# Values weighed in fp32 by two column tiles, products in another order of banks, and attention in a fixed order

## The chip, the cores and the metric

The kernel runs on one core of a Trainium2 chip. The metric is device microseconds (us) of one execution; smaller is better. The engines are named as the profile names them: PE (TensorE, matrix products), DVE (VectorE), ACT (ScalarE), POOL (GpSimd) and SP (SyncE, which issues DMAs). Products are accumulated in PSUM, which PE writes in banks of 512 fp32 columns; DVE, ACT and POOL work between PSUM and SBUF.

## The reference

Two layers of a trunk with three gated branches are applied to 512 latent tokens and 128 context tokens, 640 rows of 1024 channels. All is fp32. One layer, cut to what matters here:

```python
q, k, v, z_a, cb, cc, cx, z_b, fx, z_c, g = split(h @ w_in)
y_a = attn(q, k, v) * silu(z_a)            # 8 query heads, 2 kv heads, head_dim 64
y_b = (cb * dwconv3(cc * cx)) * silu(z_b)  # 512 channels
y_c = Re(fft2(fx)) * silu(z_c)
gates = sigmoid(g)                         # three of 1024 channels
merged = sum(gates[i] * (y_i @ w_branch[i]))
x = LN(alpha * x + gate * (merged @ w_o)) * ln_g + ln_b

# attention of a block of 128 latent queries: keys of the block, its two neighbours, and 128 cached context keys
p = softmax(concat([q @ k * 64**-0.5 (masked), sink]))[..., :-1]
y = p @ v
```

Context tokens attend to the 128 context keys of the prompt only. Keys and values of the context are outputs, too.

## The kernel before

**Precision.** Most products are made from fp32 data cut into a rounded part and a remainder, both of type fp32r; three products (high by high, high by low, low by high) stand for one. A product of 512 weight rows with 320 token columns is 12 matmuls of 128x320. The function `split` does the cut: a copy on ACT gives the high half, a subtraction on DVE the low half (L72).

**Order of work.** The kernel is written as a list of jobs. `run()` goes through it and, ahead of the jobs, loads raw weight tiles (six live at a time, on SP's queue) and splits them (five live at a time). The framework then moves instructions of an engine ahead of others where its own schedule finds that better, unless an instruction is pinned with `tc.keep_in_program_order`: pinned instructions of one engine keep the order in which the program emits them.

**Attention.** Tokens are five tiles of 128: t = 0 to 3 latent, t = 4 context. A unit is a pair (t, kv). `scores` makes, per query head g, a score block of 128 queries by W keys (W = 384, 512, 512, 384; 128 for the context) in PSUM (L651, L662), adds the mask and takes the row's maximum on DVE in one instruction (L654), makes the negated maximum nm (L669, L670), takes the exponential on ACT with a row sum (L676), and, after the reciprocal rc on DVE (L680), scales P by rc on POOL (L682). `values` turns P block by block: four transposes fill a bank (L700), `split` brings it to SBUF as pT, and two matmuls weigh it with VS, whose 128 columns are the high and the low half of 64 channels (L705, L706). The accumulated bank `po` then holds the parts by the high and the low half of the values in different partitions; ACT copies one to yt, DVE adds the other, and the result is multiplied into sz, the SiLU gate. Score, pt, po and x banks come from one pool of four banks (`aux`); scores of unit u+2 are made right after the values of unit u, so P has two buffers by unit.

**The products beside it.** Between units stand the `fills`: the products of the conv branch's input projections. A `Pair` makes two column blocks c0, c1 for 640 tokens by seven products instead of eight (sums of weights and of activations, as in Strassen's scheme). A product goes to one of three accumulators, x, y or z, and after it an evacuation follows: ACT's copy (`keep`, `last_y`) or DVE's addition (`plus`) into the rows gc and gd (gs and ga in `Gates`, a subclass of the same scheme in the gating stage that follows the Fourier stage). Accumulators y and z are halves of one tile, yz, in two banks. Sums of raw weights, s1 among them (which is accumulated by a DMA of POOL's queue), are formed on DVE. There are 8 pairs and 56 products in the attention stage of a layer.

**Output projection.** `oproj(t, n)` makes half n of 512 columns of tile t from 24 matmuls (L1185 to L1187), `residual(t, n)` adds it to x and takes statistics, `finish(t)` is the layer norm; `load_x(t)` loads x.

Of the kernel before, what the change touches and what calls it, by code (L numbers as in the profile page):

```python
# [10 lines left out]
F32R = mybir.dt.float32r  # L11
# [7 lines left out]
NT = 5  # L19
# [15 lines left out]
def body(nc, tc, I, O, ctx):  # L35
# [275 lines left out]

    def transposed(xn, nm, pin=False):
# [224 lines left out]
    def layer(l):  # L537
# [12 lines left out]
        def begin():  # L550
# [3 lines left out]
            S["VS"] = KV[:, 3072:4608].rearrange("p (b v s d) -> p b v s d", b=6, v=2, s=2)  # L554
# [36 lines left out]
        def keys_values():  # L591
# [13 lines left out]
            for i, (a, n, o) in enumerate(((0, 2, 0), (2, 3, 3))):  # L605
# [3 lines left out]
                s = pv[:, :n * 128].rearrange("p (b v d) -> p b v d", v=2, d=64)  # L609
                split(VS[:, o:o + n, :, 0], VS[:, o:o + n, :, 1], s)  # L610
            split(VS[:, 2, :, 0], VS[:, 2, :, 1], cv[:, 0:128].rearrange("p (v d) -> p v d", d=64))
# [25 lines left out]
        def scores(u):  # L637
            def body():
                t, kv = u // 2, u % 2
                nm = f"{l}{t}{kv}"  # L640
                Q, KS, P = S["Q"], S["KS"], S["P"][:, u % 2]
                tok = slice(t * 128, (t + 1) * 128)
                b0, b1 = WINDOW[t] if t < 4 else (5, 6)
                W = (b1 - b0) * 128
                keys = slice(b0 * 128, b1 * 128)
                mx = small(f"mx{nm}")
                if t < 4:
                    for g in range(4):
                        ps = aux(f"s{nm}{g}")
                        for i in range(2):  # L650
                            nc.tensor.matmul(ps[:, :W], lhsT=Q[:, kv * 4 + g, tok], rhs=KS[:, kv, i, keys],  # L651
                                             start=i == 0, stop=i == 1)
# [3 lines left out]
                                                       accum_out=mx[:, g:g + 1])  # L656
                    srcs = [P[:, g, :W] for g in range(4)]
                else:
                    ps = aux(f"s{nm}")
                    for g in range(4):  # L660
                        for i in range(2):
# [702 lines left out]
```

## Time and profile before

| what | us |
|---|---|
| median of three runs | 1288.96 (1285.04 to 1289.44) |
| the profiled execution | 1282.6 |
| its span, from first to last instruction | 1280.8 |
| PE busy | 1198.8 |
| DVE busy | 1011.1 |
| ACT busy | 622.0 |
| POOL busy | 200.1 |
| attention stage, layer 0 (110.82 to 279.78) | 168.96 |
| attention stage, layer 1 (739.44 to 904.96) | 165.52 |

The profile comes from one execution. Busy time counts an engine while an instruction of its own is being executed; on PE neighbouring matmuls overlap, so that the pitch from one start to the next is shorter than one matmul's duration. The granted clock of the whole span is 0.987 of full speed (2.4 GHz). A wait is the idle time of an engine before an instruction, put down to what released it.

### The profile page before, as it was taken

What the parts mean: (1) busy time and instruction counts of PE and PEld (TensorE: products, weight loads), DVE (VectorE), ACT (ScalarE), POOL (GpSimd) and SP (SyncE); (2) the same over time, 40 slices, a digit from 0 to 9 for tenths busy, and PEclk for the clock granted to TensorE, in tenths of its full rate; (3) what the DMA queues carried; (4) which work ended last, traced back from release to release, by engine and by line L of the source; (5) the groups of instructions that cost most, each with busy time, mean ns of one, the idle gap of its engine ahead of it and who ended that gap; (6) DMA issues with size and microseconds to landing.
All of it is one profiled execution on the core that took longest, in us unless ns stands there. A gap on an engine that the chain in (4) does not pass through costs nothing. (4 is left out here: it accounts for less than half of the span.)

```text
span 1280.8 us, 20819 instructions
## 1 busy us (share of the span) xinstructions
PE 1198.8 (94%) x7772; PEld 1134.2 (89%) x7772; DVE 1011.1 (79%) x1855; ACT 622.0 (49%) x1236; POOL 200.1 (16%) x204
## 2 busy tenths in 40 slices
PE   6999888989999999999989979998999999999997
PEld 4899778889889999999779978888999999999986
DVE  5689878868899996777777988888789974667766
ACT  4455566545544344563244656665455443446310
POOL 2011542400000000000230145241000000000001
PEclk9999999999999999999989999999999999999998
DMA  9821213243344543363412311214324533324431
GB/s 355 306 69 35 74 42 80 61 118 106 94 145 142 172 124 92 105 184 127 169 70 70 75 42 50 75 50 125 102 72 132 164 94 97 108 75 140 165 115 66
DMA packets 65812, 143.64 MB, mean 112 GB/s; under 512 B 7792, under 2 KB 8368, under 8 KB 65456
## 3 DMA queue, kind: packets, MB, share of 16 engines
q1 hardware_dynamic: 57504, 125.35, 29.4%
q0 software_dynamic: 7632, 16.68, 7.1%
q8 instruction: 61, 1.00, 0.3%
q14 instruction: 39, 0.32, 0.1%
q10 hardware_dynamic: 576, 0.30, 0.1%
HBM read 136.77 MB, written 5.52 MB: 111 GB/s over the span
## 5 line engine op out<-in xcount | busy, mean ns | idle before, releaser
L682 POOL TENSOR_SCALAR P<-P,rc 128x384 f32<-128x384 f32 (+2 forms) x80 | 114.5, 1447 | 125.5 <-DVE rc L680 98.6
L509 PE MATMUL p<-act,hlw 128*128 128x256 f32 (+1 forms) x256 | 80.5, 314 | 0.0
L511 PE MATMUL p<-act,hlw 128*128 128x256 f32 (+1 forms) x256 | 79.7, 311 | 0.0
L510 PE MATMUL p<-act,hlw 128*128 128x256 f32 (+1 forms) x256 | 79.2, 309 | 0.0
L1185 PE MATMUL o<-wo,act 128*128 128x512 f32 (+1 forms) x168 | 63.7, 381 | 2.3 <-ACT hv L331 2.3
L1186 PE MATMUL o<-wo,act 128*128 128x512 f32 (+1 forms) x168 | 63.4, 379 | 0.0
L1187 PE MATMUL o<-wo,act 128*128 128x512 f32 (+1 forms) x168 | 62.8, 380 | 0.0
L239 DVE SCALAR_TENSOR_TENSOR moda<-rawm,scond,moda 128x512 f32<-128x512 f32 x84 | 61.2, 744 | 0.4 <-DMA rawm<-in_w_mod 0.4
L69 ACT ACTIVATE gs<-y 128x320 f32<-128x320 f32 x48 | 20.9, 435 | 74.7 <-PE y L827 74.6
L509 PEld LDWEIGHTS p<-act,hlw 128*128 128x128 f32 x256 | 48.4, 189 | 1.1 <-issue 0.8
L511 PEld LDWEIGHTS p<-act,hlw 128*128 128x128 f32 x256 | 48.2, 188 | 0.0
L510 PEld LDWEIGHTS p<-act,hlw 128*128 128x128 f32 x256 | 48.2, 188 | 0.0
L75 DVE TENSOR_TENSOR gs<-pb,gs 128x640 f32<-128x640 f32 x16 | 13.2, 824 | 38.0 <-PE pb L511 38.0
L676 ACT ACTIVATE P<-P,nm 128x384 f32<-128x384 f32 (+1 forms) x64 | 42.0, 657 | 0.1
L654 DVE CUSTOM_DVE_ANT_0 P<-s,mask 128x384 f32<-128x384 f32 (+1 forms) x64 | 38.4, 615 | 3.8 <-PE s L651 3.7
L72 DVE TENSOR_TENSOR pT<-pt,pT 128x512 fp32r<-128x512 f32 x60 | 40.6, 682 | 0.6 <-ACT pT L69 0.5
L69 ACT ACTIVATE hlw<-raww 128x512 fp32r<-128x512 f32 x40 | 25.0, 631 | 32.1 <-PE p L511 19.3
L705 PE MATMUL po<-pT,KV 128*128 128x512 f32 x60 | 25.7, 428 | 15.6 <-ACT pT L69 15.5
L147 DVE TENSOR_TENSOR hlb<-rawb,hlb 128x512 fp32r<-128x512 f32 x48 | 33.0, 687 | 9.3 <-ACT hlb L69 9.1
L509 PE MATMUL pb<-sya,hlb 128*128 128x256 f32 (+1 forms) x128 | 40.1, 313 | 0.1
L69 ACT ACTIVATE hlb<-rawb 128x512 fp32r<-128x512 f32 x48 | 30.1, 627 | 20.3 <-PE z L827 8.0
L509 PE MATMUL pb<-yc,hlb 128*128 128x256 f32 (+1 forms) x128 | 39.9, 312 | 0.0
(1131 smaller groups left out, 3874.2 us busy)
## 6 DMA issues: line engine op xcount, KB each, us to landing
rawm<-in_w_mod SPq DMA_DIRECT2D x48, 512.0 KB, 5.7
rawg<-in_w_in SPq DMA_DIRECT2D x72, 256.0 KB, 3.3
rawb<-in_w_branch SPq DMA_DIRECT2D x48, 256.0 KB, 3.1
raww<-in_w_in SPq DMA_DIRECT2D x40, 256.0 KB, 4.5
rawo<-in_w_o SPq DMA_DIRECT2D x32, 256.0 KB, 4.2
rawgc<-in_w_in SPq DMA_DIRECT2D x24, 256.0 KB, 2.8
rawgd<-in_w_in SPq DMA_DIRECT2D x24, 256.0 KB, 2.9
rawgf<-in_w_in SPq DMA_DIRECT2D x24, 256.0 KB, 2.9
```

Of the source, the lines that this page charges most:

```text
L69: nc.scalar.activation(out, in_, AF.Copy)
L72: nc.vector.tensor_tensor(out=out, in0=a, in1=b, op=ALU.subtract)
L239: nc.vector.scalar_tensor_tensor(out=acc[:, c], in0=w, scalar=scond[:, k, c:c + 1], in1=acc[:, c], op0=ALU.mult, op1=ALU.add)
L509: nc.tensor.matmul(ps[:, a:b], lhsT=ld.w(0, k), rhs=mh, start=k == 0, stop=False)
L510: nc.tensor.matmul(ps[:, a:b], lhsT=ld.w(0, k), rhs=ml, start=False, stop=False)
L511: nc.tensor.matmul(ps[:, a:b], lhsT=ld.w(1, k), rhs=mh, start=False, stop=k == nk - 1)
L654: nc.vector.tensor_tensor_reduce(out=P[:, g, :W], in0=ps[:, :W], in1=mask[:, mp:mp + W], scale=1.0, scalar=-3e38, op0=ALU.add, op1=ALU.max ...
L676: nc.scalar.activation(P[:, g, :W], srcs[g], AF.Exp, scale=0.125, bias=nm_[:, g:g + 1], accum_out=sm[:, g:g + 1])
L682: nc.gpsimd.tensor_scalar(out=P[:, g, :W], in0=P[:, g, :W], scalar1=rc[:, g:g + 1], scalar2=None, op0=ALU.mult)
L1185: nc.tensor.matmul(ps, lhsT=act[:, t, 0, k], rhs=w[:, 0], start=k == 0, stop=False)
L1186: nc.tensor.matmul(ps, lhsT=act[:, t, 0, k], rhs=w[:, 1], start=False, stop=False)
L1187: nc.tensor.matmul(ps, lhsT=act[:, t, 1, k], rhs=w[:, 0], start=False, stop=k == NK - 1)
```

## The change

Five things are done.

- **Values.** VS holds plain fp32 values. One copy on ACT brings a turned block of both kv heads to pT. `weigh(b)` makes two fp32 matmuls, kv 0 and kv 1, with 64 weight columns each, placed in column tiles (0, 0) and (0, 64) of PE, into the two halves of one bank. The final multiplication reads that bank. The low half of pT (DVE), yt's copy (ACT) and addition (DVE) fall away.
- **Seven products.** Their accumulators come in the order y, z, y, x, y, z, y instead of y, x, z, y, y, y, z; the matmuls of the products of the conv pairs are pinned (those of `Gates` aren't).
- **Attention's order.** The matmuls of scores, transposes and values are pinned as well. Both units of a tile share the steps: scores (t+1, kv 0), two products, scores (t+1, kv 1), six products; then for each block b of that tile the weighing of block b-1, the transposes of b for both kv heads, and one product. P has a buffer for each kv head.
- **Conv.** The first of the three taps is scaled on ACT instead of DVE.
- **Output projection.** All of x is loaded at the begin, and residual(t, 0) follows oproj(t, 0) directly.

```diff
@@ -309,6 +309,9 @@
     def pe(ins):
         tc.keep_in_program_order(ins)
 
+    def pinned(ins):
+        tc.keep_in_program_order(ins)
+
     def transposed(xn, nm, pin=False):
         halves = []
...
@@ -563,7 +565,8 @@
 
         def begin_scores():
             P = big.tile([128, 5120], F32, name=f"P{l}", tag="C")
-            S["P"] = P[:, :4096].rearrange("p (u g k) -> p u g k", u=2, g=4)
+            S["P"] = P[:, :4096].rearrange("p (v g k) -> p v g k", v=2, g=4)
+            S["VS"] = P[:, 4096:4864].rearrange("p (b v d) -> p b v d", b=6, v=2)
         job(begin)
 
         def after_h(f):
...
-            split(VS[:, 2, :, 0], VS[:, 2, :, 1], cv[:, 0:128].rearrange("p (v d) -> p v d", d=64))
+                copy(VS[:, o:o + n], pv[:, :n * 128].rearrange("p (b v d) -> p b v d", v=2, d=64))
+            copy(VS[:, 2], cv[:, 0:128].rearrange("p (v d) -> p v d", d=64))
             nc.vector.tensor_copy(out=cv[:, 128:256], in_=pv[:, 256:384])
             nc.gpsimd.dma_start(out=O["new_v"][l], in_=cv[:, 128:256])
...
@@ -628,42 +630,52 @@
         for c in range(4):
             inproj(l, C_Q + c, use_q(c))
             if c == 0:
+                job(begin_scores)
                 job(after_h(keys_values))
             if c < len(groups):
                 job(groups[c][0])
-        job(begin_scores)
-
-
...
+        def scores(t, kv):
...
+                for i in range(2):
+                    pinned(nc.tensor.matmul(ps, lhsT=S["Q"][:, kv * 4 + g, tok], rhs=S["KS"][:, kv, i, keys],
+                                            start=i == 0, stop=i == 1))
+
+            def some(g0, g1):
+                def body():
+                    P = S["P"][:, kv]
+                    if g0 == 0:
+                        S["mx", u] = small(f"mx{nm}")
+                    for g in range(g0, g1):
                         ps = aux(f"s{nm}{g}")
-                        for i in range(2):
-                            nc.tensor.matmul(ps[:, :W], lhsT=Q[:, kv * 4 + g, tok], rhs=KS[:, kv, i, keys],
-                                             start=i == 0, stop=i == 1)
+                        score(ps[:, :W], g)
                         mp = MASKPOS[t] * 128
                         nc.vector.tensor_tensor_reduce(out=P[:, g, :W], in0=ps[:, :W], in1=mask[:, mp:mp + W],
                                                        scale=1.0, scalar=-3e38, op0=ALU.add, op1=ALU.max,
...
+                        srcs[g] = P[:, g, :W]
+                return body
...
@@ -681,36 +693,44 @@
                 for g in range(4):
                     nc.gpsimd.tensor_scalar(out=P[:, g, :W], in0=P[:, g, :W], scalar1=rc[:, g:g + 1],
                                             scalar2=None, op0=ALU.mult)
-            return body
...
+            def both(*fs):
+                return lambda: [f() for f in fs]
+            return [some(0, 2), both(some(2, 4), softmax)] if t < 4 else [both(context, softmax)]
+
+        def values(t):
+            b0, b1 = WINDOW[t] if t < 4 else (5, 6)
+            pT = {}
+
+            def turn(b):
+                pT[b] = tmp(f"pT{l}{t}{b}")
+                for kv in range(2):
+                    pt = aux(f"pt{l}{t}{b}{kv}")
                     for g in range(4):
...
+                        pinned(nc.tensor.transpose(pt[:, g * 128:(g + 1) * 128],
+                                                   S["P"][:, kv, g, (b - b0) * 128:(b - b0 + 1) * 128], ident))
+                    copy(pT[b][:, kv * 512:(kv + 1) * 512], pt)
+
+            def weigh(b):
+
+                if b == b0:
+                    S["po"] = aux(f"po{l}{t}")
+                for kv in range(2):
+                    pinned(nc.tensor.matmul(S["po"][kv * 64:(kv + 1) * 64], lhsT=S["VS"][:, b, kv],
+                                            rhs=pT[b][:, kv * 512:(kv + 1) * 512], start=b == b0, stop=b == b1 - 1,
+                                            tile_position=(0, kv * 64)))
+
+            def step(b):
+                def body():
+                    if b > b0:
+                        weigh(b - 1)
+                    if b < b1:
+                        turn(b)
+                    else:
+                        sz = S["sz"][:, :, t * 128:(t + 1) * 128]
+                        mul(sz, S["po"].rearrange("p (g q) -> p g q", g=4), sz)
+                return body
+            return [step(b) for b in range(b0, b1 + 1)]
 
         def use_za(c):
@@ -794,13 +814,15 @@
                     return lambda k, z: S["T"][i][:, z, k]
                 self.steps = [
                     (Load([s1, a11, a12, a22], [hl(a11, [], 1)]), "y", old(0, 0), self.keep(0, 0)),
+                    (Load([], [hl(s1, [], 5)]), "z", new(0), self.keep(1, 1)),
+                    (Load([], [Sum(add, s1, s1, a11), hl(s1, [], 6)]), "y", new(1), self.keep(0, 1)),
                     (Load([], [hl(a12, [], 2)]), "x", old(0, 1), self.plus(0, 0)),
-                    (Load([], [hl(s1, [], 5), Sum(add, s1, s1, a11)]), "z", new(0), lambda out: None),
-                    (Load([], [hl(s1, [], 6), Sum(sub, a11, s1, a22), Sum(add, a12, a12, s1, [s1])]), "y", new(1),
-                     self.keep(0, 1)),
-                    (Load([], [hl(a11, [a11], 7)]), "y", new(2), self.third),
-                    (Load([], [hl(a22, [a22], 4)]), "y", lambda k, z: act[:, :, z, k, 64:128], self.last_y),
-                    (Load([], [hl(a12, [a12], 3)]), "z", old(1, 1), self.last_z)]
+                    (Load([], [Sum(sub, a11, s1, a22), Sum(add, a12, a12, s1, [s1]), hl(a11, [a11], 7)]), "y", new(2),
+                     self.plus(1, 1)),
+                    (Load([], [hl(a12, [a12], 3)]), "z", old(1, 1), self.last_z),
+                    (Load([], [hl(a22, [a22], 4)]), "y", lambda k, z: act[:, :, z, k, 64:128], self.last_y)]
+
+            pin = staticmethod(pinned)
 
             def place(self, bank):
...
@@ -841,15 +863,11 @@
                     add(quarter(self.G[i], half), out, quarter(self.G[i], half))
                 return then
 
-            def third(self, out):
-                self.keep(1, 1)(out)
-                self.plus(1, 1)(self.ps["z"][:, :320].rearrange("p (t i) -> p t i", i=64))
+            def last_z(self, out):
+                self.plus(0, 1)(out)
 
             def last_y(self, out):
                 copy(quarter(self.G[1], 0), out)
-
-            def last_z(self, out):
-                self.plus(0, 1)(out)
                 self.done(*self.G)
 
@@ -864,8 +882,7 @@
                 mul(u[:, 1:513], cc[:, 0:512], cx[:, 0:512])
                 mul(u[:, 514:642], cc[:, 512:640], cx[:, 512:640])
                 y = S["cy"] = row(f"cy{l}{j}")
-                nc.vector.tensor_scalar(out=y[:, 0:641], in0=u[:, 1:642], scalar1=convw[:, l, j, 1:2], scalar2=None,
-                                        op0=ALU.mult)
+                nc.scalar.activation(y[:, 0:641], u[:, 1:642], AF.Copy, scale=convw[:, l, j, 1:2])
                 for i in (0, 2):
                     nc.vector.scalar_tensor_tensor(out=y[:, 0:641], in0=u[:, i:i + 641], scalar=convw[:, l, j, i:i + 1],
@@ -887,10 +904,15 @@
                 if fill:
                     fill.pop(0).emit(1)
 
+        def several(fs):
+            for f in fs:
+                job(f)
+
         if l == 0:
             job(groups[0][1])
-        job(scores(0))
+        several(scores(0, 0))
         gating(0)
+        several(scores(0, 1))
         if l == 0:
             job(groups[0][2])
             job(groups[1][1])
@@ -899,17 +921,19 @@
             job(groups[1][2])
         job(begin_sums)
         job(sums(0))
-        job(scores(1))
         gating(2)
         job(sums(1))
-        for u in range(10):
-            job(values(u))
-            if u == 0:
-                gating(3)
-                job(last_sum)
-            if u + 2 < 10:
-                job(scores(u + 2))
-            fills(6 if u else 2)
+        gating(3)
+        job(last_sum)
+        for t in range(NT):
+            for f in values(t):
+                job(f)
+                fills(1)
+            if t + 1 < NT:
+                several(scores(t + 1, 0))
+                fills(2)
+                several(scores(t + 1, 1))
+                fills(6)
         fills(99)
 
@@ -1030,6 +1054,8 @@
                 c = C_G + b * 8 + 2 * m
                 super().__init__(f"{l}{b}{m}", c, c + 1, begin, None)
 
+            pin = staticmethod(free)
+
             def place(self, bank):
                 return aux(f"{bank}{self.nm}")
...
@@ -1228,21 +1257,17 @@
             if l == 0:
                 job(lambda: make_h(1, t, S["xn", t], pin))
 
-        job(oproj(0, 0))
-        job(oproj(1, 0))
-        job(oproj(2, 0))
-        job(residual(0, 0))
-        job(residual(1, 0))
+        for t in range(3):
+            job(oproj(t, 0))
+        for t in range(3):
+            job(residual(t, 0))
         for t in range(NT):
-            if t > 1:
-                job(residual(t, 0))
             job(oproj(t, 1))
             job(residual(t, 1))
-            if t < NT - 2:
-                job(lambda t=t: load_x(t + 2))
             if 0 < t < NT - 1:
                 if t + 2 < NT:
                     job(oproj(t + 2, 0))
+                    job(residual(t + 2, 0))
                 next_h(t - 1)
             if t == NT - 1 and l == 0:
                 next_h(t - 1, True)
```

On PE, in the attention stage of layer 0, before: the scores of unit (2, kv 1) (s0210 to s0213; names are layer, t, kv, g) stand among the values of unit (1, kv 1) (po011) and products of the pair c01.

```order
L651 MATMUL s0210_1835<-KV0_553,Q0_552 128x512 x2
L706 MATMUL po011_1790<-pT0112_1816,KV0_553 128x512
L651 MATMUL s0211_1839<-KV0_553,Q0_552 128x512 x2
L705 MATMUL po011_1790<-pT0113_1826,KV0_553 128x512
L651 MATMUL s0212_1843<-KV0_553,Q0_552 128x512 x2
L827 MATMUL yzc01_1869<-tb0_1100,hlgc01p5_1742 128x320 x12
L827 MATMUL yzc01_1869<-tb0_1100,hlgc01p6_1759 128x320 x7
L706 MATMUL po011_1790<-pT0113_1826,KV0_553 128x512
L651 MATMUL s0213_1847<-KV0_553,Q0_552 128x512 x2
L827 MATMUL yzc01_1869<-tb0_1100,hlgc01p6_1759 128x320
L827 MATMUL xc01_1891<-act_109,hlgc01p2_1725 128x320 x12
L827 MATMUL yzc01_1869<-tb0_1100,hlgc01p6_1759 128x320 x4
```

The unit's own transposes (pt0211) stand 22 rows below the last of these, after the transposes and values of unit (2, kv 0). After, the same scores, the six products and the transposes of both kv heads:

```order
L650 MATMUL s0210_1875<-KV0_553,Q0_552 128x512 x2
L650 MATMUL s0211_1879<-KV0_553,Q0_552 128x512 x2
L650 MATMUL s0212_1883<-KV0_553,Q0_552 128x512 x2
L650 MATMUL s0213_1887<-KV0_553,Q0_552 128x512 x2
L849 MATMUL yzc01_1731<-act_109,hlgc01p3_1747 128x320 x12
L849 MATMUL yzc01_1731<-act_109,hlgc01p4_1781 128x320 x12
L849 MATMUL yzd01_1956<-act_109,hlgd01p1_1802 128x320 x12
L849 MATMUL yzd01_1956<-tb0_1132,hlgd01p5_1854 128x320 x12
L849 MATMUL yzd01_1956<-tb0_1132,hlgd01p6_1871 128x320 x12
L849 MATMUL xd01_2012<-act_109,hlgd01p2_1922 128x320 x12
L710 MATMUL pt0210_2031<-ident_90,P0_659 128x128 x4
L710 MATMUL pt0211_2037<-ident_90,P0_659 128x128 x4
```

The scores have moved from beside another unit's values to a place six products ahead of their own transposes.

On DVE, before, around the maxima of unit (2, kv 1) (P0 and mx021 from s0210): the first two rows are the sum sm020 and the reciprocal rc020 of unit (2, kv 0). The first maximum of kv 1 is the row behind the last one shown.

```order
L78 TENSOR_TENSOR sm020_1666<-sm020_1666,es020_1663 128x4
L680 RECIPROCAL rc020_1672<-sm020_1666 128x4
L78 TENSOR_TENSOR gd001_1591<-yzd00_1577,gd001_1591 128x5x64
L147 TENSOR_TENSOR hlgc01p6_1759<-rawgc01s_1390,hlgc01p6_1759 128x512
L72 TENSOR_TENSOR pT0110_1796<-pt0110_1791,pT0110_1796 128x512
L75 TENSOR_TENSOR gd001_1591<-gd001_1591,cy00_1568 128x512
L75 TENSOR_TENSOR gd001_1591<-gd001_1591,cy00_1568 128x128
L147 TENSOR_TENSOR hlgc01p7_1785<-rawgc0110_1410,hlgc01p7_1785 128x512
L72 TENSOR_TENSOR pT0111_1806<-pt0111_1801,pT0111_1806 128x512
L72 TENSOR_TENSOR pT0112_1816<-pt0112_1811,pT0112_1816 128x512
L78 TENSOR_TENSOR gd000_1590<-yzd00_1577,gd000_1590 128x5x64
L147 TENSOR_TENSOR hlgc01p4_1885<-rawgc0122_1575,hlgc01p4_1885 128x512
```

After, the same place:

```order
L681 SCALAR_TENSOR_TENSOR mx020_1805<-mx020_1805,sink_96 128x4
L147 TENSOR_TENSOR hlgd01p5_1854<-rawgd01s_1572,hlgd01p5_1854 128x512
L682 TENSOR_SCALAR nm020_1822<-mx020_1805 128x4
L72 TENSOR_TENSOR es020_1825<-sink_96,mx020_1805 128x4
L78 TENSOR_TENSOR rawgd01s_1572<-rawgd01s_1572,rawgd0110_1591 128x512
L78 TENSOR_TENSOR gc011_1745<-yzc01_1731,gc011_1745 128x5x64
L72 TENSOR_TENSOR rawgd0110_1591<-rawgd01s_1572,rawgd0122_1714 128x512
L78 TENSOR_TENSOR sm020_1828<-sm020_1828,es020_1825 128x4
L692 RECIPROCAL rc020_1834<-sm020_1828 128x4
L662 ISA P0_659,mx021_1874<-s0210_1875,mask_107 128x512
L662 ISA mx021_1874 128x1
L662 ISA P0_659,mx021_1874<-s0211_1879,mask_107 128x512
```

The maxima of kv 1 now follow rc of kv 0 directly, and the subtractions for pT (L72) are gone.

On PE, at the turn from tile 3 to tile 2's second half in layer 0's output projection, with what each row waits for, before:

```order
L318 MATMUL tr100_6506<-ident_90,xn10_6439 128x128 [waits Activation_49]
L318 MATMUL tr100_6506<-ident_90,xn10_6439 128x128 x3
L318 MATMUL tr101_6511<-ident_90,xn10_6439 128x128 [waits DVE_49]
L318 MATMUL tr101_6511<-ident_90,xn10_6439 128x128 x3
L1185 MATMUL o02512_6591<-wo02_6280,act_109 128x512 [waits Activation_49]
```

and after:

```order
L321 MATMUL tr100_6409<-ident_90,xn10_6338 128x128 [waits Activation_49]
L321 MATMUL tr100_6409<-ident_90,xn10_6338 128x128 x3
L321 MATMUL tr101_6414<-ident_90,xn10_6338 128x128 [waits DVE_49]
L321 MATMUL tr101_6414<-ident_90,xn10_6338 128x128 x3
L1214 MATMUL o02512_6489<-wo02_6172,act_109 128x512 [waits DVE_49]
```

The first matmul of o02512 waits for DVE where it waited for ACT.

## Rows read from the trace of the kernel before

**Rows 1.** The page: the span, and PE's busy time, its share and instructions.

```profile
span 1280.8 us, 20819 instructions
...
PE 1198.8 (94%) x7772; PEld 1134.2 (89%) x7772; DVE 1011.1 (79%) x1855; ACT 622.0 (49%) x1236; POOL 200.1 (16%) x204
```

**Rows 2.** Waits of PE: waiting line, releaser; total us, times, longest.

```profile
PE po L705 <- ACT pT L69: 15.5, 10, 3.8
PE yzc L827 <- ACT gc L69: 15.3, 13, 2.2
...
PE yzd L827 <- ACT gd L69: 3.8, 5, 1.0
PE y L827 <- ACT ga L69: 3.4, 4, 1.5
...
PE o L1185 <- ACT hv L331: 2.3, 2, 1.2
PE y L827 <- ACT gs L69: 2.2, 7, 0.5
```

**Rows 3.** Windows of both stages: us, each engine's busy time (x), PEclk.

```profile
110.82:279.78 168.96, 147.61 (x930) 135.94 (x928) 139.13 (x287) 99.87 (x218) 56.43 (x53) 0.99 0.26 71
739.44:904.96 165.52, 146.11 (x905) 135.09 (x903) 134.58 (x281) 98.98 (x216) 61.27 (x54) 0.97 0.26 72
```

**Rows 4.** Timeline of PE, products: start, us of the row.

```profile
1028.27 1.92 PE L827 MATMUL y<-act,hlg113p 128*128 128x320 f32 x12
1030.03 1.92 PE L827 MATMUL y<-act,hlg112p 128*128 128x320 f32 x12
```

**Rows 5.** Timeline of PE, output projection of layer 1.

```profile
1226.45 0.39 PE L1185 MATMUL o<-wo,act 128*128 128x512 f32 x1
1226.67 0.39 PE L1186 MATMUL o<-wo,act 128*128 128x512 f32 x1
```

**Rows 6.** Timeline of PE, transposes of P.

```profile
115.92 1.03 PE L700 MATMUL pt<-ident,P 128*128 128x128 f32 x8
116.71 0.37 PE L509 MATMUL p<-act,hlw 128*128 128x256 f32 x1
```

**Rows 7.** Window of the first stage, products of L827 alone.

```profile
110.82:279.78 168.96, 104.30 (x637) 96.25 (x637) 0.99 0.26 71
```

**Rows 8.** Groups by form: busy us, mean ns of one, idle before.

```profile
L682 POOL TENSOR_SCALAR P<-P,rc 128x512 f32<-128x512 f32 x32 | 54.2, 1717 | 39.6 <-DVE rc L680 20.8 <-ACT hlgd10p L69 7.4 <-ACT pT L69 4.1
...
L682 POOL TENSOR_SCALAR P<-P,rc 128x384 f32<-128x384 f32 x32 | 45.9, 1445 | 66.9 <-DVE rc L680 58.7 <-PE yzc L827 4.1 <-PE s L662 4.0
...
L72 DVE TENSOR_TENSOR pT<-pt,pT 128x512 fp32r<-128x512 f32 x60 | 40.6, 682 | 0.6 <-ACT pT L69 0.5
...
L676 ACT ACTIVATE P<-P,nm 128x512 f32<-128x512 f32 x32 | 22.6, 710 | 0.0
...
L654 DVE CUSTOM_DVE_ANT_0 P<-s,mask 128x512 f32<-128x512 f32 x32 | 21.4, 679 | 2.9 <-PE s L651 2.9
```

**Rows 9.** Timeline of PE, an fp32 product in column tiles.

```profile
80.82 0.34 PE L511 MATMUL p<-act,hlw 128*128 128x384 f32 x1
81.09 1.92 PE L464 MATMUL modp<-rawm,scond 128*32 128x512 f32 x16
82.94 0.44 PE L651 MATMUL s<-KV,Q 128*128 128x384 f32 x1
```

**Rows 10.** Timeline of VectorE, then of ACT, where Exp's table is loaded.

```profile
808.48 0.16 DVE L670 TENSOR_SCALAR nm<-mx 128x4 f32<-128x4 f32 x1
...
809.14 1.28 ACT L676 ACT_TABLE_LOAD   x1
```

**Rows 11.** Timeline of POOL, scaling of unit (1, kv 0), layer 1.

```profile
764.26 7.54 POOL L682 TENSOR_SCALAR P<-P,rc 128x512 f32<-128x512 f32 x4 [7.43 <-ACT hlgd10p L69]
```

**Rows 12.** Windows around two waits of PE: columns as in rows 3.

```profile
745.00:752.00 7.00, 3.17 (x13) 2.87 (x13) 6.01 (x11) 6.81 (x18) 2.01 (x1) 0.76 0.18 47
662.00:668.00 6.00, 6.00 (x35) 6.00 (x34) 5.46 (x9) 3.94 (x10) 3.32 (x2) 0.62 0.02 8
```

More of the change, by code (lines that the diff above doesn't have):

```diff
@@ L633, in layer, with score @@
                 job(groups[c][0])
[L634 to L648 removed]
+        def scores(t, kv):
+            u = t, kv
+            nm = f"{l}{t}{kv}"
+            tok = slice(t * 128, (t + 1) * 128)
+            b0, b1 = WINDOW[t] if t < 4 else (5, 6)
+            W = (b1 - b0) * 128
+            keys = slice(b0 * 128, b1 * 128)
+            srcs = {}
+            def score(ps, g):
+                for i in range(2):
[7 more added lines that the diff above has]
+                    for g in range(g0, g1):
                         ps = aux(f"s{nm}{g}")
[L650 to L652 removed]
+                        score(ps[:, :W], g)
                         mp = MASKPOS[t] * 128
@@ L655, in body, with context, softmax @@
                                                        scale=1.0, scalar=-3e38, op0=ALU.add, op1=ALU.max,
[L656 to L661, printed above, removed]
-                            nc.tensor.matmul(ps[:, g * 128:(g + 1) * 128], lhsT=Q[:, kv * 4 + g, tok],
-                                             rhs=KS[:, kv, i, keys], start=i == 0, stop=i == 1)
-                    nc.vector.tensor_reduce(out=mx, in_=ps.rearrange("p (g k) -> p g k", g=4),
-                                            axis=mybir.AxisListType.X, op=ALU.max)
-                    srcs = [ps[:, g * 128:(g + 1) * 128] for g in range(4)]
+                                                       accum_out=S["mx", u][:, g:g + 1])
+                        srcs[g] = P[:, g, :W]
+                return body
+            def context():
+                ps = aux(f"s{nm}")
+                for g in range(4):
+                    score(ps[:, g * 128:(g + 1) * 128], g)
+                    srcs[g] = ps[:, g * 128:(g + 1) * 128]
+                S["mx", u] = small(f"mx{nm}")
+                nc.vector.tensor_reduce(out=S["mx", u], in_=ps.rearrange("p (g k) -> p g k", g=4),
+                                        axis=mybir.AxisListType.X, op=ALU.max)
+            def softmax():
+                P, mx = S["P"][:, kv], S["mx", u]
                 nm_ = small(f"nm{nm}")
@@ L826, in body @@
                         for i, (z, y) in enumerate(((0, 0), (0, 1), (1, 0))):
-                            nc.tensor.matmul(out, lhsT=ld.w(z, k), rhs=moving(k, y), start=first and k == i == 0,
-                                             stop=k == 3 and i == 2, skip_group_check=True)
+                            self.pin(nc.tensor.matmul(out, lhsT=ld.w(z, k), rhs=moving(k, y), start=first and k == i == 0,
+                                                      stop=k == 3 and i == 2, skip_group_check=True))
                     then(out.rearrange("p (t i) -> p t i", i=64))
```

34 lines of the change are left out of this document (4 added, 30 removed).

## The prediction

> **What bounds the kernel now.** I read the head of the page first: a span of 1280.8 us with PE busy for 1198.8 of it [rows 1], so a gain must come from the 82 us in which PE is not busy, or from work that leaves PE. The waits of PE come next, since they name what PE stood for [rows 2]: values matmuls waiting for ACT's copy of pT 15.5 us, products waiting for a bank's evacuation into gc 15.3 and gd 3.8, and, in the gate pairs after the stage, ga 3.4 and gs 2.2; the output projection waits 2.3 for hv. Then the windows of the two attention stages [rows 3]: 168.96 and 165.52 us, in which PE is busy 147.6 and 146.1. Busy time overlaps between neighbouring matmuls, so I count by pitch, from start to start. Twelve 320-column matmuls take 1030.03 − 1028.27 = 1.76 us [rows 4]; a 512-column one .225 to .23 us [rows 5]; eight transposes .79 [rows 6], and with the step to their neighbours .109 each. The first stage holds 637 product matmuls [rows 7], at .1465 each 93.3 us; 120 transposes 13.1; 60 values matmuls 13.9; with the scores' 64 matmuls 12.0 and the gating projections' 49, of two widths, 7.1, at pitches between these, it comes to 139.5. PE waits some 29.5 us there, and by the same count 29.7 in the second stage, which has half of the gating. These 59 us are what the change plays for; VectorE, at 139 and 135 us of work in the two windows, is nearly as full as PE there, and I expected that to matter most.
>
> **Values.** Per block and kv head the VectorE half of the split goes: 60 × .68 = 40.6 us [rows 8]; with 20 additions of the same shape, 13.6 by the same mean, VectorE sheds 54 us; ACT loses 20 copies. Eight conv scalings leave VectorE for ACT as well. All this lies beside PE's work and is worth nothing by itself, only through waits that get shorter. On PE, 120 matmuls of .23 are replaced by 30 pairs, each pair weighing one block for both kv heads. An fp32 product in column tiles is in the trace: eight calls, 16 records, from 81.09 to the next row at 82.94 [rows 9]. That is four rounds of four tiles side by side, at most 1.85 / 4 = .46 each with the changes of tiling in them. The first record is .09 late too: the row before began at 80.82, and its 384 columns take .176 at the pitch per column of rows 4. A pair is two rounds: .92, the late start .09, and a little for an exit that is spread over four rounds there and over two here: 1.05 us, against 4 × .231 = .92. Hence +.12 × 30 = +3.7 us. From below, with nothing for changes and rounds of .43, −2; from above, if the two tiles don't run together, +26 (a rival).
>
> The Trainium skill, "TensorEngine Tiling (Array Packing)", Tiling Modes, Key Properties, says that a change of tiling mode drains TensorE, a rule against this change, which makes 60 of them; the trace agrees, with the .09 at 81.09, and by it the sum stays as it is.
>
> **The fixed order in attention.** This is the main term. Before, a unit's scores are issued two units ahead of its values and whatever is ready fills PE. The order shows unit (2, kv 1) scored, then six products, two of them already in flight, and a whole other unit's transposes before its own pt0211. After, both units of a tile are scored just ahead of it: scores kv 0, two products, scores kv 1, six products, then at once the transposes of both. PE reaches kv 1's transposes 1.85 + 3.52 + 1.85 + 10.56 + .44 = 18.2 us after it starts on kv 0's scores (eight matmuls of .231, products of 1.76, four transposes of .109).
>
> P must be ready by then. I walk the order of VectorE after the change with durations of before. kv 0: four masked maxima at .68 [rows 8], behind the scores, end at 3.7; with the gc addition, one split and two small operations, nm is there at 5.15. Exp then loads its table, 1.28 us, which needs nm: behind a split of ACT it began .5 after nm's end [rows 10], I take .25: 6.7; four exps of .71 [rows 8] end at 9.6, rc at 10.1. POOL scales four pieces, each between 1.45 (the mean at 384 keys) and 1.72 (at 512) [rows 8]: 10.3 to 16.5 at 1.55. So kv 0 is in time. But the order puts kv 0's sm and rc, which wait for these exps, ahead of kv 1's masked maxima on VectorE. These therefore begin at 10.1, not at 5.4 when their scores start; they end at 12.5, nm follows behind two splits and an addition at 15.1, exps 15.3 to 18.2, rc 18.7, scaling 18.9 to 25.0. PE stands 25.0 − 18.2 = 6.8 us. One unit of before has four scalings in 7.54 [rows 11], which would make it 8; with chains as short as the rows allow (no table, no split between) it is 4. I take 6.8 for the two tiles of 512 keys after the first, 4 for the tile of 384 (1.5 to 6: shorter maxima and exps, the same order), nothing for the context tile of 128: 17.6 a layer, 35 in all (20 to 48).
>
> Each such wait costs more than itself. Around a 3.8 us wait PE's granted clock was .76 over 7 us [rows 12], a part of it at the 1.2 GHz level: 7 × .24 = 1.7 us lost, in the window in which the wait itself lies; after a longer wait, .62 over 6 us, or 2.3 [rows 12]. Six stalls at 1.7 are 10 (5 to 20). Inside a tile, weigh(b−1) follows a product of 1.76 us after the transposes, while ACT needs two copies of .59 and may be on a split of .63: .2 us a step, 15 steps a layer, 3 us; as much again for products whose bank or split is late at the start of the stage. That is 12 for both layers (4 to 24). Stage after: 35 + 10 + 12 + 3.7 = 61, against 59 before: +2. What VectorE no longer does is not seen in it, because kv 1's chain is a chain of waits, not of work. The waits for pT (15.5) and gc in the stage do go, but they are exchanged for waits for P.
>
> **The order of products.** Between two products into one bank another bank's product now stands in most places, 1.76 us against a copy of .44. In the stage this is already in the count above; outside it, ga and gs, 3.4 + 2.2 [rows 2], go: −5.6 (−10, if waits too short for a row go as well, to +2, if splits come late in the new order: since the accumulated sum s1 is used a product earlier).
>
> **Output projection and tail.** The order shows o02512 wait for VectorE instead of ACT: two waits of 1.16 for hv [rows 2] go, −2.3 (0 to −3). The first half of tile 4's residual moves ahead of the last matmuls, −1.3, about one row-wide operation of VectorE at the end (0 to −2). All loads of x go out together and earlier, on SP's queue ahead of later weight loads: 0, or +2 if one of those comes late.
>
> **Sum.** +1.9 − 5.6 − 2.3 − 1.3 = −7.3 on the profiled execution of 1282.6 us: 1275.3. The runs' median is 1288.96, 6.4 above it, so 1281.7 as a median.
>
> **The rivals.** *The chain is shorter.* If the maxima of kv 1 don't stand behind rc for as long (kv 0's exps find their table loaded, POOL at 1.45), the stalls are 3.5, 3.5 and 2: 18 us instead of 35, with the clock's share unchanged: −17, 1265. For it: the exps of a unit can follow the unit before without another table load; against it: ACT's sigmoid work stands between units. *P is late by more, slower.* Place: POOL's scaling of kv 1 and the exps ahead of it, in the three tiles of a layer that stall. If four scalings take 7.5 instead of 6.2 [rows 11] and VectorE's queue adds another 1 us, stalls are 9, 9 and 6: +13, and if each costs 3 us of clock instead of 1.7, +8: 1281.7 + 21 = 1303. It decides from the point where each of the six stalls costs 1.2 us more than I put it, which makes the total no gain. For it: the unit at 764.26; against: most scalings in the group's mean are 1.72 and the waits for pT, as long as 3.8 today, vanish. *The column tiles don't run side by side*, since a call is two records and both of one tile may precede the other's: three rounds a pair, +.43 × 30 = +13, 1295; none together, +26, 1308. Against it, the 16 records at 81.09 stand in 1.85 us, four rounds where eight calls one after another would be 16.
>
> By the Trainium skill, "TensorE: Matmul & The Clock Gate", Part 3, The mechanism, matmuls start and end in program order without exception; records taken strictly tile by tile would then make three rounds of a pair. The records at 81.09 speak against that reading. *The products' order does nothing* (the waits for ga and gs stay): 1287, inside my forecast's own range.
>
> **Numbers.** Forecast .47, own range 1268 to 1289; shorter chain .23; later P .18; tiles not together .12. Half a per cent, about what can be told from no change here, is 6.4 us: below 1282.5, above 1295.4. Faster: .24 of the forecast's .47 and all of .23: .47. Same: .21 of the forecast, .02 and .05 of the next two: .28. Slower: .25. The range 1262 to 1303 takes in the shorter chain and the later P.
>
> **What would show it.** Right: among PE's waits the transposes of kv 1 for POOL, two long ones and a middling one per layer, in place of po for pT; po pairs about 1.05 us; rc of kv 0 just ahead of kv 1's maxima; a stage of 165 to 170 us. Wrong: no transposes that wait, stages below 160; or pairs over 1.3 us; or waits of products for their splits above 15 us, which would mean that the fixed order has moved the weight path onto PE's.

## The result, and the profile after

The changed kernel takes 1339.99 us (median of four runs, 1332.45 to 1340.15) against 1288.47: ratio 1.039, interval 1.0349 to 1.0432. It is 51.5 us slower, where 7 us less were forecast. Its profiled span is 57.5 us longer. The head of its page, as [rows 1]:

```profile
span 1338.3 us, 20691 instructions
...
PE 1225.5 (92%) x7772; PEld 1137.5 (85%) x7772; DVE 966.2 (72%) x1761; ACT 623.0 (47%) x1230; POOL 203.4 (15%) x204
```

VectorE shed its work; the span grew. To find where, I cut both executions at the same points of the program: the first product of the gate pairs in each layer, and the first transposes of P in layer 1. The windows of before (us elapsed first, then PE's busy time; PEclk behind POOL's column):

```profile
0.00:353.34 353.34, 316.63 (x2124) 289.42 (x2124) 282.40 (x578) 195.22 (x398) 80.06 (x89) 0.99 0.39 122
353.34:739.44 386.10, 374.22 (x2404) 360.80 (x2404) 317.37 (x532) 173.57 (x326) 36.93 (x35) 0.99 0.40 122
739.44:978.47 239.03, 217.56 (x1396) 204.31 (x1395) 195.96 (x399) 139.84 (x301) 67.62 (x66) 0.98 0.29 79
978.47:1280.80 302.33, 290.44 (x1855) 279.68 (x1854) 215.35 (x349) 113.41 (x211) 15.50 (x15) 0.99 0.37 114
```

and after:

```profile
0.00:376.14 376.14, 326.64 (x2124) 288.64 (x2124) 262.20 (x535) 196.32 (x395) 84.36 (x89) 0.96 0.37 117
376.14:758.03 381.89, 376.10 (x2424) 364.13 (x2425) 314.19 (x533) 174.64 (x329) 38.91 (x35) 0.99 0.40 121
758.03:1035.16 277.13, 230.51 (x1373) 202.30 (x1372) 173.99 (x351) 138.24 (x296) 64.50 (x65) 0.92 0.26 71
1035.16:1338.30 303.14, 292.28 (x1853) 282.44 (x1853) 215.83 (x345) 113.83 (x214) 15.62 (x15) 0.98 0.36 112
```

The two stretches with attention and the conv and Fourier pairs lose 22.8 and 38.1 us. Of those with gates and output projection the first wins 4.2, the second loses 0.8. PE's matmuls in the windows are the same but for 22 gating matmuls of layer 1, some 3.6 us: the change puts them ahead of the first transposes, out of the third window into the second. PE's waits, as [rows 2]:

```profile
PE yzc L849 <- DVE gc L78: 22.2, 12, 3.9
PE yzd L849 <- ACT gd L69: 18.0, 13, 3.3
PE pt L710 <- POOL P L694: 14.0, 7, 9.2
...
PE yzf L849 <- DVE fz L78: 8.4, 10, 1.0
PE yzf L849 <- ACT fz L69: 7.3, 12, 1.0
...
PE yzc L849 <- ACT gc L69: 5.2, 4, 2.0
```

With 2.8 more for yzd behind VectorE, products into yz wait 63.9 us in 55 places; before, the same kinds gave 22.2 (15.3 and 3.8 of [rows 2], 1.6 for yzd behind VectorE, 1.5 for yzf). The waits of po (17.9) and of ga, gs and hv are gone, as forecast. What PE waits for is seen at the first two products of a pair, y and then z (PE, then ACT; start, us):

```profile
260.90 1.98 PE L849 MATMUL yzc<-act,hlgc03p 128*128 128x320 f32 x12
263.46 0.85 PE L849 MATMUL yzc<-tb,hlgc03p 128*128 128x320 f32 x4 [0.59 <-ACT gc L69]
```

```profile
262.97 0.44 ACT L69 ACTIVATE gc<-yzc 128x320 f32<-128x320 f32 x1 [1.75 <-PE yzc L849]
```

The second product writes bank z, into which nothing of this pair had been written. Still it starts when ACT has copied bank y: 2.56 us after the first, where 1.76 is the pitch. All 55 waits stand ahead of the second, third, sixth and seventh product of a pair (15, 14, 12 and 14 of the 24 pairs of both layers); no first, fourth or fifth product waits. Such a wait becomes long where the evacuation itself is queued. At the next example ACT's copy stood behind the conv tap that the change had moved to ACT, and that one waited 2.9 us. The row puts this down to POOL; but the tap reads u, and VectorE, which makes u, ended it just before, at 145.89 (first row):

```profile
145.00 0.89 DVE L75 TENSOR_TENSOR u<-gc,gc 128x512 f32<-128x512 f32 x2
...
145.97 0.83 ACT L885 ACTIVATE cy<-u,convw 128x641 f32<-128x641 f32 x1 [2.88 <-POOL P L694]
146.71 0.42 ACT L69 ACTIVATE gd<-yzd 128x320 f32<-128x320 f32 x1
```

```profile
141.94 1.92 PE L849 MATMUL yzd<-act,hlgd00p 128*128 128x320 f32 x12
147.18 2.42 PE L849 MATMUL yzd<-tb,hlgd00p 128*128 128x320 f32 x12 [3.32 <-ACT gd L69]
```

### The profile page after: what moved, and what is told of

Its sections match the earlier page's. It is cut to its first block, busy times and chain, and to the rows that moved or that the text cites. A ratio compares the mean times of both kernels' runs of the same rounds, so it can differ in the third digit from the quotient of the medians.

```text
span 1338.3 us, 20691 instructions
## 1 busy us (share of the span) xinstructions
PE 1225.5 (92%) x7772; PEld 1137.5 (85%) x7772; DVE 966.2 (72%) x1761; ACT 623.0 (47%) x1230; POOL 203.4 (15%) x204
## 4 chain that ended last, share of the span: by engine, by line
PE 73%; DVE 12%; ACT 7%; issue 3%; DMA 3%; POOL 2%; DVEq 0%; POOLq 0%; ACTq 0%; SPq 0%
PE y L849 13%; PE z L849 6%; PE yzf L849 5%; PE yzc L849 5%; PE yzd L849 5%; PE pb L512 4%; PE pb L514 4%; PE pb L513 4%; PE x L849 3%; PE po L719 2%; PE p L401 2%; PE pt L710 2%; PE p L512 2%; PE p L514 2%; PE p L513 2%
## 5 line engine op out<-in xcount | busy, mean ns | idle before, releaser
L710 PEld LDWEIGHTS pt<-ident,P 128*128 128x128 f32 x240 | 26.8, 141 | 33.1 <-POOL P L694 15.8
L710 PE MATMUL pt<-ident,P 128*128 128x128 f32 x240 | 34.3, 281 | 14.0 <-POOL P L694 14.0
L69 ACT ACTIVATE pT<-pt 128x512 f32<-128x512 f32 x60 | 32.8, 593 | 23.9 <-PE pt L710 23.9
L512 PE MATMUL pb<-syb,hlb 128*128 128x256 f32 (+1 forms) x128 | 40.1, 313 | 0.0
```

The costliest lines, as they stand in the source:

```text
L69: nc.scalar.activation(out, in_, AF.Copy)
L512: nc.tensor.matmul(ps[:, a:b], lhsT=ld.w(0, k), rhs=mh, start=k == 0, stop=False)
L710: pinned(nc.tensor.transpose(pt[:, g * 128:(g + 1) * 128], S["P"][:, kv, g, (b - b0) * 128:(b - b0 + 1) * 128], ident))
```

## The experiments

Theory A: y and z are halves of one tile of PSUM, and the program orders a write to the tile behind every earlier read of it, whichever bank is read. Rivals: B, the fixed order itself; C, late P. Stalls of "76" and "29" us in the expectations are counted from start to start beyond the pitch, over 0.25 us each.

**two_tiles.** In the changed kernel:

```diff
+        turn_of = {}
...
-                    self.two = mmt(f"yz{self.nm}")
-                    return self.two[:, 0:512]
-                return self.two[:, 512:1024]
+                    self.two = mmt(f"yz{self.nm}"), mmt(f"zy{self.nm}")
+                    if turn_of.setdefault(self.nm, len(turn_of)) % 2:
+                        self.two = self.two[::-1]
+                    return self.two[0][:, 0:512]
+                return self.two[1][:, 512:1024]
```

> The changed kernel; the accumulators y and z of a conv or Fourier pair lie in two tiles of PSUM instead of two banks of one tile, and the two tiles change roles from pair to pair. Nothing else differs, and PE's order is the same. Theory A: a product into one bank waits until the other bank has been evacuated, because both banks are one tile and a write to a tile is put behind every earlier read of it; PE's stalls of over 0.25 us ahead of products into yz are 76 us in the changed kernel and 29 in the one before. Then they fall below 25 us and the time falls by 45 to 55, to 1285 to 1295 us. Rival B: the fixed order itself costs the time (nothing can move up into a wait), whatever the tiles: the stalls stay above 60 us, the time at 1325 or more. Rival C: P arrives late, which is what the prediction named: the waits of the transposes for POOL (14 us) are the larger part with what they do to the clock, and the time falls by less than 15 us.

Measured: 1294.05 (ratio to before 1.005, 1.0031 to 1.007), 46 us less than the changed kernel, with PE's order in the attention stages unchanged (around the Fourier pairs some matmuls that aren't pinned moved). All waits ahead of products into y and z fell from 63.9 to 16.5 us. The same two products now stand 1.81 us apart:

```profile
264.34 1.98 PE L853 MATMUL yzc<-act,hlgc03p 128*128 128x320 f32 x12
266.15 1.92 PE L853 MATMUL zyc<-tb,hlgc03p 128*128 128x320 f32 x12
```

Time and waits are those of theory A; B and C fall as the main cause. And the wait that the prediction had named takes part of the place, since PE now gets to the transposes sooner:

```profile
PE pt L710 <- POOL P L694: 36.9, 22, 9.2
PE zyd L853 <- ACT gd L69: 11.2, 8, 2.6
```

**products_free.** The changed kernel with

```diff
-            pin = staticmethod(pinned)
+            pin = staticmethod(free)
```

> The changed kernel with the products of the pairs not pinned; scores, transposes and values stay pinned. Theory A: the waits for the other bank stay in the program, but products of the next pair, in another tile, can move up into some of them: stalls ahead of yz products fall from 76 to about 40 us, time 1300 to 1315 us. Rival B (the fixed order): the time goes back to that of the kernel before, 1285 to 1292. Rival C (late P): no change, 1335 or more.

Measured: 1318.18 (1.0233, 1.0214 to 1.0253). The yz waits fall to 40 us, but the time stays 3 us above A's range: PE's own work grows, since products stand between the two halves of 19 of the 30 value pairs, whose starts take 51.9 us instead of 31.6 (see values_free).

**order_alone.** The kernel before with the list of seven steps, `last_z` and `last_y` of the change.

> The kernel before with only the new order of the seven products (y, z, y, x, y, z, y), nothing pinned, values as before. Theory A: four of seven products follow a product into the other half of the same tile whose evacuation they have to wait for, where it was three before (two of them into the same bank); the framework's freedom hides a part: slower by 5 to 20 us, 1293 to 1308. Prediction's reading (another bank's product covers the evacuation): faster by about 5 to 15, 1273 to 1283. Rival B (only the pins cost): the same within 5 us.

Measured: 1267.44 (0.9841, 0.9824 to 0.9858). The expectation from A is wrong: where nothing is pinned, the order is worth 21 us, more than the prediction's reading gave.

```profile
PE yzc L827 <- ACT gc L69: 9.4, 6, 3.3
...
PE po L705 <- ACT pT L69: 7.2, 6, 4.3
PE yzd L827 <- ACT gd L69: 4.6, 7, 1.4
```

With 1.7 each for yzc and yzd behind VectorE and 0.8 for yzf, yz waits 18.2 (22.2 before), po 7.6 with its second half (17.9), and ga's and gs's 5.6 are gone; waits for split weights in the gate pairs grew from 2.3 to 5.6. That is 16.6, where the two profiled spans differ by 15.9 (the medians by 21). So only 4.0 are waits of products into y and z; most is po's. What the prediction said of the order is seen in the gate pairs, where x, y and z are three tiles.

**before_two_tiles.** The kernel before with two tiles, without the change of roles.

> The kernel before with y and z in two tiles, in its own order of products (y, x, z, y, y, y, z). Theory A: of its three waits per pair two are for the same bank and stay, the last (z behind y) goes: the 29 us of stalls ahead of yz products fall by a third, time 1276 to 1282 us. Rivals B and C: nothing changes, 1285 to 1292, since in this kernel nothing is pinned and P is not late.

Measured: 1273.02 (0.9885, 0.9869 to 0.9901). The time fell by more than A said, but the yz waits didn't fall (22.3 us). The profiled spans differ by 9.5 us, of which po's waits give 3.8 (17.9 to 14.1); the rest is spread over small waits and starts, and this run alone doesn't show its mechanism.

**order_and_tiles.** Both edits in the kernel before, roles changing.

> The kernel before with the new order of the products and with y and z in two tiles that change roles from pair to pair; nothing pinned, values as before. The order alone gave 1267.4 us, two tiles alone 1273.0. If both take away the same waits (a product behind the evacuation of the pair's banks), the two together give little more than the order alone: 1260 to 1267. If the order takes away the waits for the same bank and the tiles those for the other bank, as theory A has it, the gains add: 1250 to 1258. If P's or the weights' chain is the next wait, it ends above 1265.

Measured: 1249.09 (0.9697, 0.9682 to 0.9711): 38 us, where the parts alone gave 21 and 15. They add.

**scores_together.** In two_tiles:

```diff
-            for f in values(t):
+            fs = values(t)
+            for f in fs:
                 job(f)
-                fills(1)
+                fills(1 if f is not fs[-1] else 0)
             if t + 1 < NT:
                 several(scores(t + 1, 0))
-                fills(2)
                 several(scores(t + 1, 1))
-                fills(6)
+                fills(9)
```

> The changed kernel with two tiles (1294.1 us, PE waits 36.9 us in 22 places for POOL's P), in which the scores of kv 1 follow those of kv 0 at once and nine products stand behind them (two between and six behind before; the product after a tile's last block goes there too). If P's chain is late since the maxima of kv 1 stand behind the reciprocal of kv 0 on VectorE, as the prediction walked it, the maxima come before it now and PE comes later: the waits for POOL fall below 20 us and the time to 1272 to 1282. If POOL's scaling itself (eight pieces of 1.5 to 1.7 us a tile) or ACT's exps set the end, the waits stay above 25 us and the time above 1284.

Measured: 1271.89 (0.9871, 0.9854 to 0.9888). Time and waits are as forecast, but not for the reason given. The waits for POOL fell, 11.4 of the rest at the start of layer 1's stage, 9.2 of them at one place; but VectorE's order had not changed, and the products into x now waited for score banks that kv 1's maxima held:

```profile
PE xc L853 <- DVE mx L662: 18.1, 6, 5.1
PE pt L710 <- POOL P L694: 14.7, 6, 9.2
```

**old_order_pinned.** The changed kernel with the seven steps of before.

> The changed kernel with the old order of products (y, x, z, y, y, y, z), pinned as in the change, y and z in one tile. By theory A each pair has three waits in place of four, each of an evacuation that PE can't fill: stalls ahead of yz products 55 to 70 us, time 1325 to 1338. If the new order is itself what hurts under the pins, this kernel comes back to 1300 or less. If the order is as good here as in the kernel before (21 us), it goes up to 1355 to 1365.

Measured: 1325.71 (1.0293, 1.0271 to 1.0315). In the changed kernel the new order costs 14 us; in the kernel before, with nothing pinned, it won 21. Three tile waits a pair against four: the waits into y and z are 44.6 us against 63.9, and 41 of the 43 stand ahead of the fifth, sixth and seventh product, as A has it.

**best_free.** order_and_tiles with the change's output projection and conv tap.

> The kernel with the new order and two tiles, nothing pinned, and with the change's output projection (early loads of x, residual(t, 0) right behind its product) and its conv tap on ACT. By the prediction's terms the output projection gives 2.3 us and the tail 1.3: 2 to 5 us below order_and_tiles. If the free schedule takes the gain back elsewhere: the same within 2 us.

Measured: 1243.82 (0.9655, 0.9639 to 0.9672), 5.3 us less. The output projection gives about what was forecast here, 3.8 us of the profiled spans' 5.0 behind the first gate products; what the conv tap does wasn't run by itself.

**maxima_first.** In scores_together, softmax(kv 0) and softmax(kv 1) both behind the maxima of both units, and tile 0's scores of both ahead of the first gating product.

> As scores_together (1271.9 us, waits for POOL 14.7, x products behind VectorE's maxima 18.1), with the softmax of both units emitted behind the maxima of both, in tile 0 too (there both units' scores stand ahead of the first gating product). On VectorE the maxima of kv 1 then stand ahead of kv 0's sum and reciprocal, which wait for ACT's exps. If that place in VectorE's queue is what delays kv 1, as the prediction said, the x products' waits for the score banks go (18.1 to under 5) and the waits for POOL fall below 8: 1245 to 1256 us. If the maxima wait for something else, both stay and the time stays at 1265 or more.

Measured: 1275.72 (0.9898, 0.9875 to 0.9921). Half right, and 20 us above the forecast: the x waits are gone, so VectorE's queue caused those. The waits for POOL rose to 24.5, so P was not late for that reason alone: POOL's eight scalings of a tile take this long in one go,

```profile
810.19 16.55 POOL L694 TENSOR_SCALAR P<-P,rc 128x512 f32<-128x512 f32 x8 [11.01 <-DVE es L72]
```

2.07 us each; the mean of all 32 of this size is 1.98, against 1.72 before [rows 8].

**x_beside_z.** In best_free:

```diff
                 if bank == "x":
-                    return aux(f"x{self.nm}")
+                    return self.two[1][:, 0:512]
```

> best_free (1243.8 us) with accumulator x in the spare bank of z's tile instead of the pool of four banks that scores, transposes and values share. By the tile rule x and z don't get in each other's way, since a product into y stands between them each time; the shared pool has one tile less to serve. Waits of scores, transposes and x for that pool are small here (under 3 us): 0 to 5 us faster, 1239 to 1244. If x behind z waits after all: slower, 1248 or more.

Measured: 1231.07 (0.9554, 0.9527 to 0.958), 12.8 us less than best_free and more than expected; the fastest kernel of the study. Waits into y and z fell from 13.1 to 7.1 us; why the gain is larger than forecast wasn't separated. Of them only the second row here is longer than 1 us in all:

```profile
PE po L705 <- ACT pT L69: 4.8, 4, 1.9
PE yzc L831 <- ACT gc L69: 4.7, 3, 2.4
```

**maxima_first_x.** The same edit in maxima_first.

> maxima_first with x in the spare bank of z's tile. If the shared pool of four banks still holds products up there, 3 to 10 us faster than maxima_first, 1238 to 1250; if the queue of VectorE was the whole reason, the same within 2 us.

Measured: 1280.48 (0.9924, 0.9895 to 0.9952), no gain. The waits for POOL are still 23.1 us; that late P sets the pace is likely, but not shown.

**values_free.** The changed kernel with the edits of two_tiles, products_free and x_beside_z.

> The changed kernel with all its parts (fp32 values in column tiles, both units of a tile together, output projection), y and z in two tiles, x in the spare bank of z's, and the products not pinned: what the change gives once the banks no longer hold products up and PE may fill waits. x_beside_z, which has the old values and the old order of attention, took 1231.1 us. In this program the framework puts other instructions between the two matmuls of 21 of the 30 pairs; such a half then runs by itself, about 2 us a pair instead of 1.05, some 20 us in all. If that and the late P are what is left of the change's cost: 1250 to 1268 us. If VectorE's relief (54 us of work less) is worth something once nothing else holds PE: below 1240. If the pins alone hid the rest: the same as x_beside_z within 5 us.

Measured: 1293.46 (1.0059, 1.0034 to 1.0083), 62 us above x_beside_z. That is more than expected. From each start to the next, PE's value matmuls take 60.5 us, 5.4 of it waits that follow them, against 31.6 in the changed kernel: one half of a pair by itself takes 1.00 us,

```profile
169.95 1.07 PE L719 MATMUL po<-pT,P 128*64 128x512 f32 x2
170.95 1.09 PE L710 MATMUL pt<-ident,P 128*128 128x128 f32 x8
```

and PE waits 10.8 us for POOL. The rest of the 62 was not separated. Attention is still pinned here; fp32 values in a kernel with nothing pinned were not run, so that their own worth stays open.

## Why the prediction was wrong

**The step that failed** is "The order of products": "Between two products into one bank another bank's product now stands in most places, 1.76 us against a copy of .44. In the stage this is already in the count above". The count had 12 us for waits inside the tiles of attention, and only half of them, 3 us a layer, for products whose bank or split is late. Measured: 63.9, of it 48.2 in the conv pairs and 15.7 in the Fourier pairs. The condition was not another bank but another tile. By banks, each of the seven has another product between itself and the evacuation that it needs; by tiles, four of them start behind one with nothing between. Where PE had nothing else to do there, it mostly stood idle for .53 us at least (.59 in the rows above, a start .8 late), and longer where ACT or VectorE stand at exps or at rc. Two_tiles shows it with PE's order in attention unchanged: 46 of the 51.5 us. The pins make the rule dear: nothing can move into the wait (products_free gives 22 us back, in spite of broken pairs). The order's effect is −21 in the kernel before, where nothing is pinned, and +14 in the changed one; since these differ in more than the pins, that the pins alone turn its sign isn't shown. The pairs of the Fourier stage, pinned as well, had no term at all.

The 59 us that the change was to play for were mis-sized, too: they are the windows less pitches, and the waits of PE in these two windows come to 21.0 and 19.2. The other 19 were starts slower than the pitches taken.

**Hidden in the trace of before.** The kernel's waits for gc and gd [rows 2] were read as waits for one bank. A look at which bank the waiting product wrote, and which one the copy read, would have shown the difference. The last two products of a pair, y and then z, show it in the kernel before (PE, then ACT): z starts when bank y has been copied.

```profile
270.64 1.92 PE L827 MATMUL yzc<-act,hlgc03p 128*128 128x320 f32 x12
273.09 2.02 PE L827 MATMUL yzc<-act,hlgc03p 128*128 128x320 f32 x12 [0.53 <-ACT gc L69]
```

```profile
272.60 0.44 ACT L69 ACTIVATE gc<-yzc 128x320 f32<-128x320 f32 x1 [1.08 <-PE yzc L827]
```

**P late.** Forecast 35 us in six places. In the changed kernel 14.0, of which 11.4 stand at the start of layer 1's stage, where I had none; at the forecast places PE comes late itself. With two tiles 36.9 in 22 waits: again 11.4 there, and 24.5 at the six places, 3.8, 6.5 and 1.4 in layer 0 and 4.0, 7.5 and 1.4 in layer 1, where 6.8, 6.8 and 4 were forecast. So mechanism and size were near, as the next wait and not the first. Two causes are seen, the maxima of kv 1 behind rc of kv 0, which the walk had, and POOL's pace; their shares weren't separated.

**Values.** Forecast 1.05 us a pair. Starts of all 30 pairs take 31.6 us, 1.05 each on average and 1.01 in 25 of them, with each pair in one piece:

```profile
286.02 1.08 PE L719 MATMUL po<-pT,P 128*64 128x512 f32 x4
287.03 0.41 PE L849 MATMUL yzd<-tb,hlgd03p 128*128 128x320 f32 x1
```

One half by itself takes 1.00 (values_free). So the tiles run side by side, and the rival of three or four rounds falls. The 120 matmuls before took 33.8 us by their starts, waits left out, not 27.7, so that +3.7 came out as −2.2. VectorE's busy time fell by 44.9 us; what that relief is worth no run shows by itself.

**Clock.** Forecast 10 us for it. PEclk of the two stretches with attention went from 0.99 and 0.98 to 0.96 and 0.92, a larger share of them at the 1.2 GHz level. By 376 × .03 and 277 × .06 that is some 28 us of the 61 lost there, an estimate that counts time in which PE waits, too; PE's busy time in the same rows grew by 10.0 and 13.0 us. In two_tiles the clock of the whole span is .974, between the .965 of the changed kernel and the .987 of before.

**Gates, output projection, tail.** Forecast −9.2; the two windows from the first gate products on changed by −4.2 and +0.8, the first with 22 gating matmuls more. The waits named did go, ga and gs (5.6) and hv (2.3). But the gate pairs' accumulator y now waits for splits 5.5 us instead of 2.3, and 4.4 for ACT's copies into fy, the rows of the Fourier transform:

```profile
PE y L849 <- ACT fy L69: 4.4, 2, 2.2
...
PE y L849 <- ACT hlg111p L69: 2.4, 1, 2.4
PE y L849 <- ACT hlg011p L69: 2.4, 1, 2.4
```

So the terms were right as waits and not as a gain: what the gate pairs' y waits in all went from 7.9 to 9.9.

**Conv tap.** Counted only as VectorE's relief, with no cost on ACT. It put a wait for VectorE's u into ACT's queue ahead of evacuations (7.5 us of idle time of ACT in eight taps), which is a wait that the change adds and that I didn't follow.

## What to carry to other kernels

Before counting on two banks to overlap, see whether the program keeps them apart: in the trace, a product that writes one bank and starts with the end of a copy of the other says that it doesn't. An order that won in a kernel where the framework may fill waits cost time in one where it is pinned; take the dependencies away first, then fix the order. The kernel with two accumulators in two tiles, the third beside the one that is never its neighbour, the products free in the new sequence, and the output projection and the conv tap of the change is 57 us faster than the kernel before: the sequence alone gave 21, the two tiles 15 to 18, and the third accumulator's place 13.

## What was not expected of the hardware

Half of an fp32 pair in column tiles costs nearly the whole: 1.00 us alone, 1.01 for both in most places. POOL's scaling of 128x512 took a mean of 1.72 us in the kernel before and 1.98 in maxima_first, 2.07 in the run of eight shown; what slows it was not tried.
